# Three-block model, last block: gates and outputs with tokens on partitions, tanh gates in the recurrent layer, and down projections over both activation parts at once

## The chip, the cores and the metric

The kernel runs on one core of one Trainium2 chip. The metric is device microseconds of one execution, the median of several runs. TensorE (PE) multiplies, its weight loads (PEld) overlap it; VectorE (DVE), ScalarE (ACT), GpSimd (POOL) and SyncE (SP, which issues most of the loads) work beside it.

## What is computed

One sequence of 256 tokens (272 with 16 meta tokens in the first part) and 1024 channels, in float32, passes through three blocks. The first has an attention layer and a gated linear recurrent layer; the second has two hybrid layers (sparse attention, a long convolution, a short one, three gates, a feed-forward part with a convolution); the third has retention and block attention behind two sigmoid gates, and a feed-forward part of 2816 channels. What the change touches:

```python
# recurrent layer of block 1
r = jax.nn.sigmoid(jnp.einsum('btgi,gij->btgj', ub, w_rg).reshape(B, T, LRU_WIDTH) + b_rg)
i = jax.nn.sigmoid(jnp.einsum('btgi,gij->btgj', ub, w_ig).reshape(B, T, LRU_WIDTH) + b_ig)
log_a = -LRU_C * r.astype(jnp.float32) * jax.nn.softplus(-lam.astype(jnp.float32))
a = jnp.exp(log_a)
mult = jnp.sqrt(-jnp.expm1(2.0 * log_a))
...
b = mult * (i * uc).astype(jnp.float32)
...
# feed-forward part of block 2, both layers
return x + (jax.nn.silu(u_gate) * u_val) @ w_down
...
# block 3
ret = jax.nn.silu(rg) * retention(rq, rk, rv)
a = ret @ w_ret_out[l]
...
b = moba_attention(mq, mk, mv) @ w_moba_out[l]
mix = jax.nn.sigmoid(ga) * a + jax.nn.sigmoid(gb) * b
x = x + mix @ w_o[l]
h2 = rmsnorm_3(x, norm2_w[l])
f = (jax.nn.silu(h2 @ w_ffn_gate[l]) * (h2 @ w_ffn_up[l])) @ w_ffn_down[l]
x = x + f
```

## The kernel before

**Products in three parts.** Every large product is made of float32 numbers split in two: a high part in TensorE's fp32r format and the low rest. `mm3` adds up high weight x high activation, low x high and high x low, three matmuls for each 128 channels of the contraction (one step of k). Weights arrive in units of at most 1024 columns (`raw`, a load that SP issues); `emit_unit` makes the high part `whi` on ACT (L175) and the low part `wlo` on DVE (L181). Units are emitted three ahead of their use (`AHEAD = 3`, five buffers each). Activations are split in the same way by `split` (L157, L158) and `split_scaled` (L161, L162).

**Two forms of a product.** In the channel form (`tile_fm`, `part`) a 128 x 128 piece of the weight is loaded into TensorE and the activation streams through, with 256 columns (tokens; 272 in block 1); one output tile has 128 channels on partitions and takes one PSUM bank. In the token form (`tok_group`, `proj_tok`) 128 tokens of the activation are loaded and 512 columns of the weight stream; a group makes 512 channels for both halves of the tokens and takes two banks. Seven banks rotate. The hybrid layers' gates and outputs are in the token form; there `to_fm` turns a result back with TensorE transposes, four for a pair of channel tiles, and `mixture` does that while other matmuls run. In block 3 the projections `w_t3` are in the token form; the gates `w_g3`, the outputs `w_mo` and `w_ro`, and `w_o3` are in the channel form.

**What sets the order.** One stream of instructions is written out by hand; generators (norms, attention, the recurrence) are started with `spawn` and stepped by `tick`, once per eight steps of k times a rate; `drain` runs a generator to its end. The Tile scheduler then orders each engine's queue; `late` pins an instruction, and each engine runs its queue in order.

**Places that the change touches.** `lru()`: `block` (gate activations, L719), `gates` (exp, tanh and the input multiply, L709 to L712), the square root (L725), `conv4`, `chain` (L740 to L747: rr, the multiply on POOL L743, the scan), and `gated` (L766). Its products are `w_b_in` (16 tiles), `w_b_g` (4 units) and `w_b_out`; `yh`, `yl` are the parts of the activation of `w_b_out`. Tables of functions are loaded on ACT before a function of another table. `hybrid()` ends with `ffn` and a `residual` over `w_dn`, 8 tiles of 22 steps of k, whose activation parts are `fh` and `fl`. `third()`: `norm` makes the norm's scale per token (`rcol`) and, as a row over all partitions, `rb`; `retain` computes one head of the retention and turns it back (`rt`, L1466) into `rT`; the gate loop; `residual` over `w_o3`; `ffn`; and the last projection `w_d3`, with the addition (L1546) and the store of each tile.

The loop of the gates before:

```python
for m in range(8):
    o = self.tile_fm("w_g3", 16 - 8 * b + m, 8, xs, T)
    g = self.small("g3")[:, :T]
    dve.tensor_mul(g, o, rb)
    act.activation(g, g, AF.Sigmoid)
    ...
    o = self.tile_fm(wn, m, kt, ys, T)
```

Of the kernel before, what the change touches and what calls it, by code (L numbers as in the profile page):

```python
# [18 lines left out]
T = 256  # L19
# [36 lines left out]
class _Null:  # L56
# [14 lines left out]
    def __exit__(self, *a):  # L71
        return False


class Prog:
# [142 lines left out]
    def tile_fm(self, name, m, kt, xs, t):  # L218

        o = self.acc()[:, :t]  # L220
        for k0 in range(0, kt, 8):
            k1 = min(kt, k0 + 8)
            self.part(o, self.unit(name, m, k0 * 128, (k1 - k0) * 128), xs, k0, k1, kt, k0)
        return o

# [198 lines left out]
    def decay_rate(self):  # L424
# [19 lines left out]
        v.tensor_scalar_mul(self.spm8, al, -8.0)  # L444
        v.tensor_scalar_mul(self.sp4, al, 4.0)
# [228 lines left out]
    def residual(self, name, kt, xs, x, t, t0, gains, g2=None, lead=(2, 6), between=None):  # L674
# [8 lines left out]
        first = self.lead_fm(name, range(nl), xs, n, lead[1], between)  # L683
        for m in range(8):
            o = next(first) if m < nl else self.tile_fm(name, m, kt, xs, n)
            src = x[:, m, t0:]
            dve.tensor_add(src, o, src)
# [7 lines left out]
    def lru(self):  # L695
# [10 lines left out]
        def gates(g):  # L706

            for i in (2 * g, 2 * g + 1):
                self.late(act.activation(aa[:, i], rr[:, i], AF.Exp,  # L709
                                         scale=self.spm8[:, i:i + 1]))  # L710
                last[0] = act.activation(rr[:, i], rr[:, i], AF.Tanh, scale=self.sp4[:, i:i + 1])
                dve.tensor_mul(ii[:, i], ii[:, i], uc[:, i])  # L712

        def block(g):
            for c, o in self.tiles_of_unit("w_b_g", g, 4, 2,
                                           lambda k: (uh[:, 2 * g + k], ul[:, 2 * g + k]), T1):
                i = 2 * g + c % 2
                dst, b = (rr, "b_b_rg") if c < 2 else (ii, "b_b_ig")
                self.late(act.activation(dst[:, i], o, AF.Sigmoid, bias=self.v(b, i)))  # L719
            if g % 2:  # L720
# [4 lines left out]
                self.after(act.activation(rr[:, c], rr[:, c], AF.Sqrt), last[0])  # L725
# [196 lines left out]
    def hybrid(self, layer):  # L922
# [339 lines left out]
        fz = [(self.big("fh", 8, T, F32R), self.big("fl", 8, T, F32R)) for _ in range(3)]  # L1262
# [11 lines left out]
        def finish(og, ou, i):  # L1274
# [4 lines left out]
            self.split(fz[i // 8][0][:, i % 8], fz[i // 8][1][:, i % 8], u)  # L1279
# [3 lines left out]
        self.residual("w_dn_" + L, 22, lambda k: (fz[k // 8][0][:, k % 8], fz[k // 8][1][:, k % 8]),  # L1283
                      x, T, 0, nxt)
# [34 lines left out]
    def third(self):  # L1319
# [15 lines left out]
        def group(g):  # L1335
# [6 lines left out]
            self.proj_tok("w_t3", g, 512, dst)  # L1342
# [86 lines left out]
        rT = self.big("rT", 8, T)  # L1429

        def retain(hd):
# [32 lines left out]
            for i in range(2):  # L1464
                for j in range(2):
                    te.transpose(pt[:, i * 256 + j * 128:i * 256 + j * 128 + 128],  # L1466
                                 y[:, j * 256 + i * 128:j * 256 + i * 128 + 128], self.ident)
            act.activation(rT[:, 2 * hd:2 * hd + 2], pt.rearrange("p (a t) -> p a t", a=2),
                           AF.Copy)
# [10 lines left out]
        def norm():  # L1480
            yield
            self.norm_cols("n31")
            yield
            return (yield from self.rows(self.rcol, SEG2, "rb31"))

        job = self.spawn(norm(), 0.7)
        group(0)
        group(1)
        rb = self.drain(job)
# [9 lines left out]
        gr = self.big("gr", 8, T)  # L1499
        for m in range(8):  # L1500
            o = self.tile_fm("w_g3", m, 8, xs, T)
            dve.tensor_mul(gr[:, m], o, rb)
# [4 lines left out]
        def gated():  # L1507
            for m in range(8):
                dve.tensor_mul(rT[:, m], rT[:, m], gr[:, m])
                self.split(rT_h[:, m], rT_l[:, m], rT[:, m])  # L1510
                yield

        mg = self.big("mg3", 8, T)
# [196 lines left out]
```

## Time and profile before

| | |
|---|---|
| median of 3 runs | 1733.04 us (1731.53 to 1735.68) |
| profiled execution | 1733.38 us, of which the span is 1731.3 us |
| PE busy | 1709.9 us, 99%, 12215 matmuls |
| PEld busy | 1622.9 us, 94% |
| DVE busy | 1365.5 us, 79% |
| ACT busy | 1068.0 us, 62% |
| POOL busy | 61.7 us, 4% |
| HBM | 293.96 MB read, 170 GB/s over the span |

Busy time is the time in which at least one instruction of the engine ran. Matmuls are pipelined, so that one starts long before the last has ended; the pace of TensorE is the step from one start to the next. Instructions are named by line, engine, operation and out<-in in the program's names. The time in brackets behind an instruction is the idle time of its engine just before it, with what ended it. The granted clock is the share of 2.4 GHz that TensorE was given.

### The profile page before, as it was taken

What the parts mean: (1) busy time and instruction counts of PE and PEld (TensorE: products, weight loads), DVE (VectorE), ACT (ScalarE), POOL (GpSimd) and SP (SyncE); (2) the same over time, 40 slices, a digit from 0 to 9 for tenths busy, and PEclk for the clock granted to TensorE, in tenths of its full rate; (3) what the DMA queues carried; (4) which work ended last, traced back from release to release, by engine and by line L of the source; (5) the groups of instructions that cost most, each with busy time, mean ns of one, the idle gap of its engine ahead of it and who ended that gap; (6) DMA issues with size and microseconds to landing.
All of it is one profiled execution on the core that took longest, in us unless ns stands there. A gap on an engine that the chain in (4) does not pass through costs nothing.

```text
span 1731.3 us, 31869 instructions
## 1 busy us (share of the span) xinstructions
PE 1709.9 (99%) x12215; PEld 1622.9 (94%) x12215; DVE 1365.5 (79%) x2943; ACT 1068.0 (62%) x1808; POOL 61.7 (4%) x92
## 2 busy tenths in 40 slices
PE   9999899999999999999999999999999999999999
PEld 8999899998888999999999888999998789999999
DVE  7769998998997998667998898898757677786553
ACT  5667775677656776546578557576545756455442
POOL 1000100000000000000000000000000000000000
PEclk9999999999999999999999999999999999999999
DMA  7425465776775555667686775656665436656563
GB/s 271 135 71 170 133 204 177 218 221 195 230 227 176 191 180 181 184 175 210 190 228 196 214 222 189 202 171 197 186 191 187 146 96 187 189 163 196 184 184 97
DMA packets 91545, 318.64 MB, mean 184 GB/s; under 512 B 10448, under 2 KB 11616, under 8 KB 91392
## 3 DMA queue, kind: packets, MB, share of 16 engines
q1 hardware_dynamic: 84384, 292.51, 53.1%
q0 software_dynamic: 7008, 24.09, 7.0%
q8 instruction: 96, 1.57, 0.4%
q14 instruction: 57, 0.47, 0.1%
HBM read 293.96 MB, written 1.05 MB: 170 GB/s over the span
## 4 chain that ended last, share of the span: by engine, by line
PE 92%; ACT 3%; DVE 2%; issue 1%; DMA 1%; SPq 0%; DVEq 0%; POOLq 0%; ACTq 0%
PE acc L205 22%; PE acc L207 22%; PE acc L206 21%; PE tok L207 7%; PE tok L205 7%; PE tok L206 7%; DVE wlo L181 1%; ACT whi L175 1%; PE lg L1115 1%; PE ix L1070 1%; PE po L1108 1%; DMA wlo<-raw 1%; ACT ca L1234 0%; DMA raw<-w_a_in 0%; PE pt L913 0%
## 5 line engine op out<-in xcount | busy, mean ns | idle before, releaser
L175 ACT ACTIVATE whi<-raw 128x1024 fp32r<-128x1024 f32 (+3 forms) x573 | 586.4, 1027 | 417.1 <-PE acc L207 170.3
L181 DVE TENSOR_TENSOR wlo<-raw,whi 128x1024 fp32r<-128x1024 f32 (+3 forms) x531 | 628.3, 1186 | 203.6 <-ACT whi L175 199.3
L205 PE MATMUL acc<-bh,whi 128*128 128x256 f32 x1600 | 459.1, 288 | 0.0
L206 PE MATMUL acc<-bh,wlo 128*128 128x256 f32 x1600 | 451.7, 283 | 0.0
L207 PE MATMUL acc<-bl,whi 128*128 128x256 f32 x1600 | 451.2, 283 | 0.0
L205 PEld LDWEIGHTS acc<-bh,whi 128*128 128x128 f32 x1600 | 306.8, 192 | 2.7 <-issue 1.4
L206 PEld LDWEIGHTS acc<-bh,wlo 128*128 128x128 f32 x1600 | 306.6, 192 | 2.2 <-issue 0.7
L207 PEld LDWEIGHTS acc<-bl,whi 128*128 128x128 f32 x1600 | 306.1, 192 | 0.2 <-DVE bl L158 0.2
L979 DVE SCALAR_TENSOR_TENSOR ca<-apad,vec,ca 128x226 f32<-128x226 f32 (+14 forms) x480 | 195.9, 460 | 0.3
L206 PE MATMUL acc<-ah,wlo 128*128 128x256 f32 (+1 forms) x528 | 151.5, 287 | 6.1 <-DVE wlo L181 6.1
L205 PE MATMUL acc<-ah,whi 128*128 128x256 f32 (+1 forms) x528 | 153.3, 290 | 1.5 <-ACT ah L161 1.1
L207 PE MATMUL acc<-al,whi 128*128 128x256 f32 (+1 forms) x528 | 151.5, 287 | 0.0
L205 PE MATMUL acc<-fh,whi 128*128 128x256 f32 x528 | 149.4, 283 | 0.0
L206 PE MATMUL acc<-fh,wlo 128*128 128x256 f32 x528 | 149.4, 283 | 0.0
L207 PE MATMUL acc<-fl,whi 128*128 128x256 f32 x528 | 149.4, 283 | 0.0
L206 PEld LDWEIGHTS acc<-ah,wlo 128*128 128x128 f32 x528 | 101.2, 192 | 7.1 <-DVE wlo L181 7.0
L205 PEld LDWEIGHTS acc<-ah,whi 128*128 128x128 f32 x528 | 101.2, 192 | 2.3 <-ACT ah L161 1.3
L205 PE MATMUL tok<-whi,ah 128*128 128x424 f32 (+1 forms) x272 | 102.7, 377 | 0.0
L205 PEld LDWEIGHTS acc<-fh,whi 128*128 128x128 f32 x528 | 101.4, 192 | 0.0
L206 PEld LDWEIGHTS acc<-fh,wlo 128*128 128x128 f32 x528 | 101.4, 192 | 0.0
L207 PEld LDWEIGHTS acc<-fl,whi 128*128 128x128 f32 x528 | 101.4, 192 | 0.0
L207 PEld LDWEIGHTS acc<-al,whi 128*128 128x128 f32 x528 | 101.1, 192 | 0.2 <-DVE al L162 0.2
(559 smaller groups left out, 3332.8 us busy)
## 6 DMA issues: line engine op xcount, KB each, us to landing
raw<-w_up SPq DMA_DIRECT2D x88, 512.0 KB, 3.9
raw<-w_g SPq DMA_DIRECT2D x72, 512.0 KB, 4.4
raw<-w_c SPq DMA_DIRECT2D x48, 512.0 KB, 4.5
raw<-w_f SPq DMA_DIRECT2D x44, 512.0 KB, 3.6
wlo<-raw POOLq DMA_DIRECT2D x36, 512.0 KB, 6.6
raw<-w_t SPq DMA_DIRECT2D x40, 424.0 KB, 3.2
raw<-w_a SPq DMA_DIRECT2D x32, 512.0 KB, 4.4
raw<-w_dn SPq DMA_DIRECT2D x32, 512.0 KB, 3.6
```

Source lines behind the costliest of these rows:

```text
L175: nc.scalar.activation(hi[:, c], raw[:, c], AF.Copy)
L181: nc.vector.tensor_sub(lo[:, c], raw[:, c], hi[:, c].bitcast(F32))
L205: mm(out, wh, xh, start=start, stop=False)
L206: mm(out, wl, xh, start=False, stop=False)
L207: mm(out, wh, xl, start=False, stop=stop)
L979: tap = dve.scalar_tensor_tensor(ca[:, i, d:], ga[:, i, :T - d], w(i, j), ca[:, i, d:], op0=ALU.mult, op1=ALU.add)
L1070: te.matmul(ps[:, n * 2 * nk:(n + 1) * 2 * nk].rearrange("p (h k) -> p h k", h=2), kiT[:, 2 + i, q], kiT[:, 6:8, :nk], start=True, stop=True)
L1108: te.matmul(po, tok[k][:, 584 + g * 128:584 + (g + 1) * 128], ptb[:, k * n:(k + 1) * n], start=k == 0, stop=k == j)
L1115: te.matmul(ps[:, i * nk:(i + 1) * nk], qT[:, h, q], kiT[:, g, :nk], start=True, stop=True)
```

## The change

It has three parts.

In `lru()` the two sigmoids are written as tanh of half the argument. `spm8` and `sp4` are halved and serve as scale and bias, the square root takes a scale of 0.25, the first token's multiplier is 0.5, and the input multiply adds 1. The multiply by rr in `chain` moves from POOL to DVE.

For the three projections with 22 steps of k (`w_dn` in both hybrid layers, `w_d3`) the activation's high and low part lie beside each other (`Pairs`), so that the high weight takes both in one matmul of 512 columns; the low weight takes the high part with 256. The output has two halves in one bank, which are added to x one after the other.

In `third()` the gates `w_g3` and the outputs `w_mo` and `w_ro` get the token form (their weights are laid out anew on the host). The norm's scale is applied on ACT per token (`rcol`), so `rb` and its row matmuls go. `retain` writes the token-major `ry`, and `gated` multiplies and turns it back with `to_fm`; the mixture `mg` is turned back by `mixture`, during the last output groups and, for the last four channel tiles, between the two halves of the first four tiles of `w_o3` (`lead=(4, 4)`).

```diff
+class Pairs:
+    def __init__(self, prog, name, t):
+        self.a = [prog.big(name + "%d" % i, 8, t, F32R) for i in range(2)]
+    def __call__(self, k):
+        i = 2 * (k % 4)
+        return self.a[k // 4][:, i:i + 2]
...
+    def wide_part(self, o, unit, xs, k0, k1, kt, base=0):
+        wh, wl = unit
+        mm = self.nc.tensor.matmul
+        for k in range(k0, k1):
+            x = xs(k)
+            c = slice((k - base) * 128, (k - base + 1) * 128)
+            mm(o, wh[:, c], x, start=k == 0, stop=k == kt - 1, skip_group_check=True)
+            mm(o[:, 0], wl[:, c], x[:, 0], start=False, stop=k == kt - 1, skip_group_check=True)
+        self.tick((k1 - k0) / 8)
...
-        v.tensor_scalar_mul(self.spm8, al, -8.0)
-        v.tensor_scalar_mul(self.sp4, al, 4.0)
+        v.tensor_scalar_mul(self.spm8, al, -4.0)
+        v.tensor_scalar_mul(self.sp4, al, 2.0)
+        self.hb = cp.tile([128, 16], F32, name="hb")
+        v.tensor_scalar_mul(self.hb, self.v("b_b_rg", 0, 16), 0.5)
...
         for m in range(8):
-            o = next(first) if m < nl else self.tile_fm(name, m, kt, xs, n)
             src = x[:, m, t0:]
+            if wide:
+                o = next(first) if m < nl else self.wide_fm(name, m, kt, xw, n)
+                dve.tensor_add(src, o[:, 1], src)
+                o = o[:, 0]
+            else:
+                o = next(first) if m < nl else self.tile_fm(name, m, kt, xs, n)
             dve.tensor_add(src, o, src)
...
-                self.late(act.activation(aa[:, i], rr[:, i], AF.Exp,
-                                         scale=self.spm8[:, i:i + 1]))
-                last[0] = act.activation(rr[:, i], rr[:, i], AF.Tanh, scale=self.sp4[:, i:i + 1])
-                dve.tensor_mul(ii[:, i], ii[:, i], uc[:, i])
+                s8, s4 = self.spm8[:, i:i + 1], self.sp4[:, i:i + 1]
+                self.late(act.activation(aa[:, i], rr[:, i], AF.Exp, scale=s8, bias=s8))
+                last[0] = act.activation(rr[:, i], rr[:, i], AF.Tanh, scale=s4, bias=s4)
+                dve.scalar_tensor_tensor(ii[:, i], ii[:, i], 1.0, uc[:, i], op0=ALU.add,
+                                         op1=ALU.mult)
...
-                self.late(act.activation(dst[:, i], o, AF.Sigmoid, bias=self.v(b, i)))
+                self.late(act.activation(dst[:, i], o, AF.Tanh, scale=0.5,
+                                         bias=self.hb[:, b + i:b + i + 1]))
...
-                self.after(act.activation(rr[:, c], rr[:, c], AF.Sqrt), last[0])
+                self.after(act.activation(rr[:, c], rr[:, c], AF.Sqrt, scale=0.25), last[0])
...
-                dve.memset(rr[:, i, 0:1], 1.0)
-                pool.tensor_mul(ii[:, i], ii[:, i], rr[:, i])
+                dve.memset(rr[:, i, 0:1], 0.5)
+                dve.tensor_mul(ii[:, i], ii[:, i], rr[:, i])
...
-            y = self.half_k("gny")
             for j in range(2):
-                c = slice(j * 256, j * 256 + 256)
-                act.activation(y[:, c], po[:, c], AF.Identity, scale=r[:, j:j + 1],
-                               bias=nm[:, j:j + 1])
-            yield
-            pt = self.acc("rt")
...
+                act.activation(ry[:, j, e], po[:, j * 256:j * 256 + 256], AF.Identity,
+                               scale=r[:, j:j + 1], bias=nm[:, j:j + 1])
...
-            return (yield from self.rows(self.rcol, SEG2, "rb31"))
...
+                dve.tensor_mul(ry[:, :, c], ry[:, :, c], gr[:, :, c])
                 yield
+                self.to_fm(ry, m, rT_h, rT_l)
...
+            for g in range(2):
+                c = slice(g * 512, g * 512 + 512)
+                o = self.tok_group("w_g3", 4 - 2 * b + g, 8, xs)
+                sgs = [self.half_k("sgt") for _ in range(2)]
+                for j in range(2):
+                    act.activation(sgs[j], o[j], AF.Sigmoid, scale=self.rcol[:, j:j + 1])
...
+                if b == 1 and g == 0:
+                    self.drain(rjob)
+                    rjob = self.spawn(self.mixture(mg, mixed, mh, ml))
+                o = self.tok_group(wn, g, kt, ys)
...
+        self.residual("w_o3", 8, lambda k: (mh[:, k], ml[:, k]), x, T, 0, ["norm2_w_3"],
+                      lead=(4, 4), between=lambda: self.drain(rjob))
...
         for m in range(8):
-            o = self.tile_fm("w_d3", m, 22,
-                             lambda k: (fz[k // 8][0][:, k % 8], fz[k // 8][1][:, k % 8]), T)
-            dve.tensor_add(x[:, m], o, x[:, m])
+            o = self.wide_fm("w_d3", m, 22, lambda k: fz[k // 8](k % 8), T)
+            dve.tensor_add(x[:, m], o[:, 1], x[:, m])
+            dve.tensor_add(x[:, m], o[:, 0], x[:, m])
             nc.sync.dma_start(self.out[:, m], x[:, m])
```

PE's queue at the end of the last projection, the last two steps of k, before:

```order
L205 MATMUL acc<-fh,whi 128x256
L206 MATMUL acc<-fh,wlo 128x256
L207 MATMUL acc<-fl,whi 128x256
L205 MATMUL acc<-fh,whi 128x256
L206 MATMUL acc<-fh,wlo 128x256
L207 MATMUL acc<-fl,whi 128x256
L1703 UNCONDITIONAL_BRANCH
```

The same place after the change:

```order
L250 MATMUL acc<-f_17488,whi 128x512
L251 MATMUL acc<-f_17488,wlo 128x256
L250 MATMUL acc<-f_17488,whi 128x512
L251 MATMUL acc<-f_17488,wlo 128x256
L1771 UNCONDITIONAL_BRANCH
```

Two matmuls stand for three, the first of twice the width.

DVE's queue in the recurrent layer, between the low weight parts of two tiles of `w_b_in`, before (uc<-aa,ii is the scan, gy<-acc the eviction of a gate tile):

```order
L181 TENSOR_TENSOR wlo<-raw,whi 128x1024
L740 SCALAR_TENSOR_TENSOR rr<-aa,rr 128x272
L771 TENSOR_TENSOR gy<-acc,nb_1932 128x256
L742 MEMSET rr 128x1
L740 SCALAR_TENSOR_TENSOR rr<-aa,rr 128x272 x2
L742 MEMSET rr 128x1
L747 SCALAR_TENSOR_TENSOR uc<-aa,ii 128x272
L774 SCALAR_TENSOR_TENSOR gy<-th,gy 128x256
L747 SCALAR_TENSOR_TENSOR uc<-aa,ii 128x272
L742 MEMSET rr 128x1
L740 SCALAR_TENSOR_TENSOR rr<-aa,rr 128x272
L181 TENSOR_TENSOR wlo<-raw,whi 128x1024
```

The same stretch after the change:

```order
L197 TENSOR_TENSOR wlo<-raw,whi 128x1024
L832 TENSOR_TENSOR gy<-acc,nb_1934 128x256
L801 SCALAR_TENSOR_TENSOR rr<-aa,rr 128x272 x2
L803 MEMSET rr 128x1
L801 SCALAR_TENSOR_TENSOR rr<-aa,rr 128x272
L804 TENSOR_TENSOR ii<-ii,rr 128x272
L803 MEMSET rr 128x1 x2
L808 SCALAR_TENSOR_TENSOR uc<-aa,ii 128x272
L835 SCALAR_TENSOR_TENSOR gy<-th,gy 128x256
L832 TENSOR_TENSOR gy<-acc,nb_1934 128x256
L804 TENSOR_TENSOR ii<-ii,rr 128x272
L197 TENSOR_TENSOR wlo<-raw,whi 128x1024
```

Two multiplies (ii<-ii,rr) and a second eviction stand in it now; one scan and one rr have moved behind the second wlo, ahead of the first `yl`.

PE's queue in the first half of `w_o3` after the change, where the last eight transposes of `mg` stand between the fourth and the fifth step of k of the leading tiles:

```order
L221 MATMUL acc<-mh,whi 128x256
L222 MATMUL acc<-mh,wlo 128x256
L223 MATMUL acc<-ml,whi 128x256
L919 MATMUL tr<-ident,mg_16575 128x128 x8
L221 MATMUL acc<-mh,whi 128x256
L222 MATMUL acc<-mh,wlo 128x256
```

Before, the outputs `rT` were followed by the matmuls of `w_o3` alone.

## Rows read from the trace of the kernel before

**Rows 1.** The page: busy us (share) and instructions; chain that ended last.

```profile
PE 1709.9 (99%) x12215; PEld 1622.9 (94%) x12215; DVE 1365.5 (79%) x2943; ACT 1068.0 (62%) x1808; POOL 61.7 (4%) x92
PE 92%; ACT 3%; DVE 2%; issue 1%; DMA 1%; SPq 0%; DVEq 0%; POOLq 0%; ACTq 0%
```

**Rows 2.** Groups (xcount, busy us, mean ns) and timeline (start us, us), last projection.

```profile
L205 PE MATMUL acc<-fh,whi 128*128 128x256 f32 x528 | 149.4, 283 | 0.0
...
1664.11 0.28 PE L205 MATMUL acc<-fh,whi 128*128 128x256 f32 x1
...
1727.35 0.28 PE L207 MATMUL acc<-fl,whi 128*128 128x256 f32 x1
```

**Rows 3.** Timeline, PE, two token groups of a hybrid layer, 48 matmuls, ends.

```profile
478.75 0.39 PE L206 MATMUL tok<-whi,ol 128*128 128x512 f32 x1
...
489.40 0.39 PE L205 MATMUL tok<-whi,bh 128*128 128x512 f32 x1
```

**Rows 4.** Windows: stretch, us, busy of PE, PEld, DVE, ACT, POOL; PEclk; DMA.

```profile
140.00:216.00 76.00, 68.96 (x538) 67.47 (x537) 68.97 (x151) 57.46 (x95) 7.84 (x8) 0.98 0.46 145
```

**Rows 5.** Timeline, PE waits in the recurrent layer; then a window there.

```profile
185.18 0.38 PE L206 MATMUL acc<-ah,wlo 128*128 128x256 f32 x1 [1.88 <-DVE wlo L181]
...
204.17 0.39 PE L206 MATMUL acc<-ah,wlo 128*128 128x256 f32 x1 [3.05 <-DVE wlo L181]
...
210.73 0.39 PE L207 MATMUL acc<-yl,whi 128*128 128x256 f32 x1 [1.26 <-DVE yl L162]
...
186.00:200.00 14.00, 14.00 (x108) 14.00 (x108) 11.02 (x23) 13.77 (x22) 0.83 (x1) 0.89 0.60 186
```

**Rows 6.** Timeline, DVE: two operations in a row; the last addition.

```profile
155.78 0.78 DVE L158 TENSOR_TENSOR ul<-uc,uh 128x272 fp32r<-128x272 f32 x2
...
1727.66 0.42 DVE L1546 TENSOR_TENSOR x<-acc,x 128x256 f32<-128x256 f32 x1 [7.49 <-PE acc L207]
```

**Rows 7.** Groups of PE from 1398.46 to 1512.85 us, gates and outputs.

```profile
L205 PE MATMUL acc<-ah,whi 128*128 128x256 f32 x192 | 55.3, 288 | 0.0
...
L205 PE MATMUL acc<-rTh,whi 128*128 128x256 f32 x64 | 18.1, 283 | 0.0
...
L205 PE MATMUL acc<-bT,whi 128*128 128x256 f32 x32 | 9.1, 285 | 0.0
```

**Rows 8.** Timeline, PE, four transposes of the retention among matmuls.

```profile
1428.40 0.28 PE L207 MATMUL acc<-al,whi 128*128 128x256 f32 x1
1428.52 0.60 PE L1466 MATMUL rt<-ident,gny 128*128 128x128 f32 x4
1428.88 0.36 PE L205 MATMUL acc<-ah,whi 128*128 128x256 f32 x1
1429.08 0.28 PE L206 MATMUL acc<-ah,wlo 128*128 128x256 f32 x1
```

**Rows 9.** Timeline, PE, the row broadcast of block 3's first norm.

```profile
1318.04 0.61 PE L312 MATMUL rb31rp<-rb31dg,ones 128*128 128x128 f32 x4
```

**Rows 10.** Groups from 176 to 212 us; then timeline of POOL and DVE.

```profile
L181 DVE TENSOR_TENSOR wlo<-raw,whi 128x1024 fp32r<-128x1024 f32 x9 | 12.0, 1332 | 0.0
...
L740 DVE SCALAR_TENSOR_TENSOR rr<-aa,rr 128x272 f32<-128x272 f32 x8 | 5.0, 647 | 0.8 <-ACT rr L725 0.8
...
L771 DVE TENSOR_TENSOR gy<-acc,nb 128x256 f32<-128x256 f32 x8 | 3.3, 418 | 2.9 <-PE acc L207 2.9
...
202.16 0.88 POOL L743 TENSOR_TENSOR ii<-ii,rr 128x272 f32<-128x272 f32 x1 [1.02 <-DVE rr L742]
...
202.34 1.77 DVE L181 TENSOR_TENSOR wlo<-raw,whi 128x1024 fp32r<-128x1024 f32 x1
...
204.38 1.21 DVE L181 TENSOR_TENSOR wlo<-raw,whi 128x1024 fp32r<-128x1024 f32 x1
```

**Rows 11.** Timeline, ACT, recurrent layer: exp, tanh and a table load.

```profile
167.52 0.53 ACT L709 ACTIVATE aa<-rr,spm 128x272 f32<-128x272 f32 x1
...
168.27 0.51 ACT L711 ACTIVATE rr<-rr,sp 128x272 f32<-128x272 f32 x1
...
183.90 1.28 ACT L709 ACT_TABLE_LOAD   x1
```

More of the change, by code (lines that the diff above doesn't have):

```diff
@@ L224, in tile_fm, with wide_fm, wide_lead @@
         return o
+    def wide_part(self, o, unit, xs, k0, k1, kt, base=0):
[7 more added lines that the diff above has]
+        self.tick((k1 - k0) / 8)
+    def wide_fm(self, name, m, kt, xs, t):
+        o = self.acc()[:, :2 * t].rearrange("p (a t) -> p a t", a=2)
+        for k0 in range(0, kt, 8):
+            k1 = min(kt, k0 + 8)
+            self.wide_part(o, self.unit(name, m, k0 * 128, (k1 - k0) * 128), xs, k0, k1, kt, k0)
+        return o
+    def wide_lead(self, name, ms, xs, t, ks, between=None):
+        os = [(self.acc()[:, :2 * t].rearrange("p (a t) -> p a t", a=2),
+               self.unit(name, m, 0, 1024)) for m in ms]
+        for o, u in os:
+            self.wide_part(o, u, xs, 0, ks, 8)
+        if between:
+            between()
+        for o, u in os:
+            self.wide_part(o, u, xs, ks, 8, 8)
+            yield o
     def lead_fm(self, name, ms, xs, t, ks, between=None):
@@ L1259, in hybrid @@
                       [("norm2_g_2", layer)], lead=(4, 4), between=lambda: self.drain(job))
-        fz = [(self.big("fh", 8, T, F32R), self.big("fl", 8, T, F32R)) for _ in range(3)]
+        fz = [Pairs(self, "f", T) for _ in range(3)]
         def conv3(o, c):
@@ L1333, in third, with group @@
         t1 = [self.big("t1_%d" % j, 1, 2048)[:, 0] for j in range(2)]
-        def group(g):
+        os = []
+        def group(g, wait=True):
             if g < 4:
@@ L1341, in group, with evict @@
                 dst = lambda j: rv[:, j, (g - 5) * 512:(g - 4) * 512]
-            self.proj_tok("w_t3", g, 512, dst)
+            os.append((self.tok_group("w_t3", g, 8, xs), dst))
+            if wait:
+                evict(g)
+        def evict(g):
+            o, dst = os[g]
+            for j in range(2):
+                act.activation(dst(j), o[j], AF.Copy, scale=self.rcol[:, j:j + 1])
             done[0] = g + 1
@@ L1482, in norm @@
             self.norm_cols("n31")
[L1483 to L1484 removed]
         job = self.spawn(norm(), 0.7)
[L1487 removed]
+        group(0, wait=False)
+        self.drain(job)
+        evict(0)
         group(1)
[L1489 removed]
         ajob = self.spawn(attention(), 1.2)
@@ L1497, in third @@
         rjob = self.spawn(self.stagger([retain(i) for i in range(4)], 3), 1.0)
[L1499 to L1502, printed above, removed]
+        gr = self.big("gr", 2, 1024)
+        for g in range(2):
+            o = self.tok_group("w_g3", g, 8, xs)
+            for j in range(2):
+                act.activation(gr[:, j, g * 512:g * 512 + 512], o[j], AF.Copy,
+                               scale=self.rcol[:, j:j + 1])
         self.drain(ajob)
@@ L1536, in finish @@
+                mixed[0] = b * (g + 1)
+        self.residual("w_o3", 8, lambda k: (mh[:, k], ml[:, k]), x, T, 0, ["norm2_w_3"],
+                      lead=(4, 4), between=lambda: self.drain(rjob))
+        fz = [Pairs(self, "f", T) for _ in range(3)]
         def finish(og, ou, i):
```

67 lines of the change are left out of this document (31 added, 36 removed).

## Prediction

> **What bounds the kernel now.** The page's busy list comes first [rows 1]: TensorE is busy for 1709.9 of the 1731.3 us and DVE for 1365.5. The second line there, the chain of work that ended last, puts 92% of the span on PE. So the time is, nearly everywhere, the number of matmuls times the step from one start to the next, and other engines matter only where PE stands still for them. The busy share itself is no measure of speed, since the matmuls overlap (283 ns each by the page [rows 2], yet one starts every 120 ns); the steps are read from starts in the timeline.
>
> The step comes next. In the last down projection the 528 matmuls of 256 columns start between 1664.11 and 1727.35 us without a gap [rows 2]: 63.24 / 527 = 0.1200 us a step. With 512 columns, in the token-on-partition groups of the hybrid layers, 47 steps take 489.40 - 478.75 us [rows 3]: 0.2266 us, 0.2267 below. Twice the columns thus cost 0.1067 us more, and 0.0133 us of every step is there whatever the width. A pair of 256-column matmuls (0.2400) that becomes one of 512 gives back 0.0133 us.
>
> Last, the places where PE stands still and which the change touches. In the stretch from 140 to 216 us, which holds the recurrent layer, PE is busy for 68.96 of 76 us and DVE for 68.97 [rows 4]. PE's rows there [rows 5] wait 1.88 and 3.05 us for `wlo`, the low part of a weight that DVE makes, and 1.26 us for `yl`. In 186 to 200 us the granted clock is 0.89 (a part of that at the lower level, 1.2 of 2.4 GHz), right after the 1.88 us wait; 0.11 x 14 us = 1.5 us more. After the 3.05 us wait it did not fall.
>
> **The change part by part.** *Down projections.* Per step of k there are now three matmuls of 256 columns, 0.3600 us. Afterwards one of 512 (the high weight on both activation parts) and one of 256 (the low weight), 0.2267 + 0.1200 = 0.3467. There are 3 projections x 8 tiles x 22 steps = 528 steps (the page's x528 of [rows 2]); all lie on the path. 528 x 0.0133 = **-7.0 us**. The evictions double (two additions instead of one, both on DVE), 24 additions at about 0.36 us, hidden by the 7.6 us of the next tile. Only the very last one is not: x of the last tile is ready one addition later, **+0.35** (one such addition takes 0.42 alone, two operations of that kind in a row 0.78 [rows 6], so 0.36 for one more).
>
> *Last block, gates and outputs.* Before, 192 + 64 + 32 matmuls of 256 columns for each of the three products [rows 7], 864 in all. Afterwards the activations are the loaded side and the weights stream at 512 columns: 432 matmuls. 432 x 0.0133 = **-5.8 us**. Weights, bytes and splits are the same in amount.
>
> *Transposes.* Token-major results have to be turned back. 16 transposes of the retention's output go, 16 of `ry` and 16 of `mg` come: 16 more. Four of them between two matmuls of 256 columns shift the start of the second matmul behind from 0.24 to 1429.08 - 1428.40 = 0.68 us [rows 8]: 0.44 us for four, 0.11 each. 16 x 0.11 = **+1.8 us**. The row broadcast of the first norm (`rb31`, four short matmul records [rows 9]) goes; by the price of four transposes **-0.4**.
>
> *Cover of the new transposes.* The last eight of `mg` stand, after the change, behind 48 matmuls of w_o3 (48 x 0.12 = 5.8 us). That hides four DVE operations of 512 columns on the last outputs, under 0.7 us each by the 1.21 us of 1024 columns [rows 10]: 2.8 us at most, ahead of the first of the eight transposes. Without that cover they would cost 2.8 us. I take nothing, with +3 as the bad end. The gates' evictions move to ACT with a scale per token and get fewer (16 small DVE multiplies and 16 sigmoids become 8 sigmoids of twice the width), so no engine has more to do there.
>
> *Recurrent layer.* The sigmoids become tanh, which lies in one table with exp: aa (exp) at 167.52 and rr (tanh) at 168.27 follow with no load between [rows 11]. Three loads like the one at 183.90 go, 3 x 1.28 = 3.8 us of ACT. That is not on PE's path by itself; it lets the square root, and with it DVE's chain of rr, ii and uc, begin earlier. DVE decides here. It gains eight multiplies that GpSimd did: 8 x 0.36 = +2.9 us. It loses what GpSimd did to it: while GpSimd multiplies (202.16), the wlo at 202.34 takes 1.77 us against 1.21 for the one at 204.38. The group rows show the same: rr L740 has a mean of 647 ns and wlo 1332 [rows 10]. That is 0.5 us for each of the eight, -4.0 to -4.5. Of its waits in that stretch, 2.9 us for PE and 0.8 for ACT [rows 10], I let half go, since DVE is behind PE more often afterwards: -1.8. DVE reaches the first `yl` some 3 us sooner. But DVE is still the later one: in the new order a multiply and one more eviction stand ahead of the second late wlo, and a multiply, a scan and an rr ahead of the first `yl`. PE gets to its last wait earlier and stands longer there, and a fall of the clock as above would take 1.5 us back. Bounds: -5 (all waits and the fall gone) and +1 (the eight multiplies come on top, no wait goes, a second fall). I take **-2.5**, nearer to DVE's 3 us than to the middle.
>
> Sum: -7.0 + 0.35 - 5.8 + 1.8 - 0.4 - 2.5 = -13.5 us. The profiled execution took 1733.38 us, 2.1 more than its span; the median of the runs is 1733.04, 0.3 lower. 1733.04 - 13.5 = **1719.5 us**.
>
> **The rivals.** *The recurrent layer gives nothing or loses.* For it: DVE is as busy as PE there and gets more instructions; against it: the stretched rows. Then -11 to -10, 1722 to 1723.
>
> *The fixed part does not halve.* A 512-column matmul is followed in the down projections by a short one with other weights, a mix that no row shows; if the short one had to wait for its weights, or if the 13 ns belonged to something other than the matmul, the 12.8 us would shrink. By [rows 2, 3] it is part of every step, and the groups of [rows 3] load weights for each matmul too. The Trainium skill (TensorE: Matmul & The Clock Gate, section Back-to-back issue gap) gives columns / 2.4 GHz + 2.5 ns for matmuls back to back, so only 2.5 ns would be saved on each of the 960: 2.4 us. This trace does not agree (13.3 ns beyond columns / 2.4 GHz at both widths). If only a fifth of the gain came, the sum would be -13.5 + 10.4, 1729.9.
>
> *Slower: the two-bank groups make PE wait.* A token group holds two accumulators until ACT or DVE, busy with weight splits, have emptied them, and seven are in rotation with the transposes. It costs one wait per group, 10 groups from the first gate to the last output; from 13.5 / 10 = 1.35 us per group on it decides, and at 1.7 us a group the time is 1733.04 - 13.5 + 17 = 1736.5. Against it: the same form runs in the hybrid layers with no gap over the 47 steps of [rows 3], across the border between two groups.
>
> *It does not do what it says*: the tanh form might keep its loads; the built order has four loads in that stretch instead of seven, so no.
>
> **How the numbers follow.** Forecast (-16 to -12) 0.64; recurrent layer without gain 0.22; a few us of new waits in the last block (1725 to 1729) 0.06; fixed part stays 0.05; slower 0.03. What a measurement of this kernel can tell from no change is about 0.2%, 3.5 us. Faster 0.93 (the forecast, the recurrent layer without gain, the new waits, and a hundredth of the fixed-part case), same 0.04 (the rest of that case), slower 0.03. The range takes the recurrent layer from -5 to +1, the cover's +3 and the spread of the runs: 1714.5 to 1726.
>
> **What would show it.** In the profile after: the f matmuls of 512 and 256 columns with a step of 0.347 us for two, 61.0 us instead of 63.4 for the last projection; the stretch from the first gate to w_o3 some 3.5 us shorter, with no wait over 0.5 us ahead of the `mg` transposes; wlo in the recurrent stretch at 1.2 us throughout, rr near 0.43, and less time between the first late wlo and `yl`. Wrong if the two-matmul step is over 0.355 us, if `tok` matmuls of the last block wait for ACT or DVE, or if PE waits over 8 us in the recurrent layer.

## The result and the profile after

The changed kernel takes 1722.88 us (median of 4 runs, 1721.77 to 1723.06); the kernel before took 1733.52 us beside it (4 runs, 1731.53 to 1735.68). The ratio is 0.9939, with a 95% interval of 0.9928 to 0.9951: faster by 10.6 us. The forecast was 1719.5 us, 13.5 less than before. Direction and range held; the gain is some 3 us smaller than forecast.

The profiled execution after took 1721.77 us with a span of 1720.0, 11.3 less than the span before; it lies 1.1 us under the median of the runs. From its page come the busy engines and the chain of work that ended last, as in [rows 1], and the two groups that take the place of the groups of [rows 2]:

```profile
PE 1702.6 (99%) x11267; PEld 1573.6 (91%) x11267; DVE 1360.3 (79%) x2922; ACT 1064.5 (62%) x1784; POOL 53.8 (3%) x84
...
PE 91%; ACT 4%; DVE 2%; DMA 1%; issue 1%; SPq 0%; POOLq 0%; ACTq 0%; DVEq 0%
...
L250 PE MATMUL acc<-f,whi 128*128 128x512 f32 x528 | 186.7, 399 | 0.0
L251 PE MATMUL acc<-f,wlo 128*128 128x256 f32 x528 | 148.3, 281 | 0.0
```

PE is still busy 99% of the span and the chain still runs on it. Of the 11.3 us, 7.3 are busy time of PE and 4.0 idle time; PE's waits in the recurrent layer (7.0 us before and 2.9 after, from 176 to 212 us) make up nearly all of the idle part. Where the 11.3 us come from is split with seven starts. Timeline of PE, kernel before: first matmul of the recurrent layer's gates, of its output projection, of the first hybrid layer, of the last block, of the retention, of w_o3 and of the last feed-forward part.

```profile
155.75 0.29 PE L205 MATMUL acc<-uh,whi 128*128 128x272 f32 x1
206.97 0.28 PE L205 MATMUL acc<-yh,whi 128*128 128x256 f32 x1
233.14 0.36 PE L205 MATMUL tok<-whi,ah 128*128 128x424 f32 x1
1301.23 0.40 PE L205 MATMUL tok<-whi,ah 128*128 128x512 f32 x1
1402.61 0.38 PE L1433 MATMUL rs<-qkT 128*128 128x256 f32 x1
1512.90 0.28 PE L205 MATMUL acc<-mh,whi 128*128 128x256 f32 x1
1535.94 0.28 PE L205 MATMUL acc<-ah,whi 128*128 128x256 f32 x1
```

The same places in the timeline of the changed kernel:

```profile
155.54 0.29 PE L221 MATMUL acc<-uh,whi 128*128 128x272 f32 x1
199.76 0.28 PE L221 MATMUL acc<-yh,whi 128*128 128x256 f32 x1
228.33 0.36 PE L221 MATMUL tok<-whi,ah 128*128 128x424 f32 x1
1294.31 0.40 PE L221 MATMUL tok<-whi,ah 128*128 128x512 f32 x1
1395.17 0.38 PE L1502 MATMUL rs<-qkT 128*128 128x256 f32 x1
1501.24 0.28 PE L221 MATMUL acc<-mh,whi 128*128 128x256 f32 x1
1525.41 0.28 PE L221 MATMUL acc<-ah,whi 128*128 128x256 f32 x1
```

The differences of neighbouring starts, after less before:

| stretch | before, us | after, us | difference |
|---|---|---|---|
| up to the gates | 155.75 | 155.54 | -0.2 |
| recurrent layer up to its output projection | 51.22 | 44.22 | -7.0 |
| that projection | 26.17 | 28.57 | +2.4 |
| two hybrid layers (with two of the down projections) | 1068.09 | 1065.98 | -2.1 |
| last block up to the retention | 101.38 | 100.86 | -0.5 |
| retention, gates, outputs | 110.29 | 106.07 | -4.2 |
| w_o3 | 23.04 | 24.17 | +1.1 |
| from there to the end of the span | 195.4 | 194.6 | -0.8 |

The last row holds the third down projection (-1.2) and the added addition behind the last matmul (+0.4). The last projection itself, timeline of PE in the changed kernel:

```profile
1653.57 0.40 PE L250 MATMUL acc<-f,whi 128*128 128x512 f32 x1
1653.80 0.28 PE L251 MATMUL acc<-f,wlo 128*128 128x256 f32 x1
1653.92 0.40 PE L250 MATMUL acc<-f,whi 128*128 128x512 f32 x1
1654.16 0.28 PE L251 MATMUL acc<-f,wlo 128*128 128x256 f32 x1
1654.28 0.40 PE L250 MATMUL acc<-f,whi 128*128 128x512 f32 x1
1654.52 0.28 PE L251 MATMUL acc<-f,wlo 128*128 128x256 f32 x1
1654.63 0.40 PE L250 MATMUL acc<-f,whi 128*128 128x512 f32 x1
...
1715.64 0.28 PE L251 MATMUL acc<-f,wlo 128*128 128x256 f32 x1
```

Three steps of k (a 512-column and a 256-column matmul each) take 1654.63 - 1653.57 = 1.06 us, 0.3533 a step. The forecast was 0.3467 and the step before was 0.3600, so half of the gain came. The starts in the trace repeat every third step: 241 and 120 ns, 236 and 113, 232 and 118. From first to last start it is 62.07 us where [rows 2] have 63.24.

The recurrent layer, windows of the changed kernel (columns as in [rows 4]), then PE's two waits behind 200 us in its timeline:

```profile
140.00:216.00 76.00, 72.96 (x577) 71.88 (x576) 69.22 (x164) 56.14 (x96) 0.00 (x0) 0.98 0.49 157
...
200.00:212.00 12.00, 9.01 (x56) 8.21 (x55) 11.85 (x28) 3.99 (x9) 0.00 (x0) 0.86 0.47 163
...
201.37 0.38 PE L222 MATMUL acc<-yh,wlo 128*128 128x256 f32 x1 [0.45 <-DVE wlo L197]
...
204.67 0.39 PE L223 MATMUL acc<-yl,whi 128*128 128x256 f32 x1 [2.49 <-DVE yl L178]
```

The waits of 1.88 and 3.05 us for `wlo` in [rows 5] are gone. The wait for `yl` grew from 1.26 to 2.49 us, and the lower level of the clock (1.2 GHz) stands behind it now (0.86 over the 12 us: 1.7 us lost) instead of in 186 to 200 us. GpSimd does nothing in the stretch any more. DVE's groups from 176 to 212 us (count, busy us, mean ns), which answer to [rows 10]:

```profile
L197 DVE TENSOR_TENSOR wlo<-raw,whi 128x1024 fp32r<-128x1024 f32 x11 | 13.3, 1215 | 0.0
...
L801 DVE SCALAR_TENSOR_TENSOR rr<-aa,rr 128x272 f32<-128x272 f32 x8 | 3.3, 436 | 0.6 <-ACT rr L786 0.6
```

`wlo` fell from 1332 to 1215 ns and `rr` from 647 to 436.

In the last block, the last eight transposes of `mg`, PE's timeline:

```profile
1506.87 0.28 PE L223 MATMUL acc<-ml,whi 128*128 128x256 f32 x1
1506.99 1.03 PE L919 MATMUL tr<-ident,mg 128*128 128x128 f32 x8
1507.79 0.36 PE L221 MATMUL acc<-mh,whi 128*128 128x256 f32 x1
1507.99 0.28 PE L222 MATMUL acc<-mh,wlo 128*128 128x256 f32 x1
1508.28 0.38 PE L221 MATMUL acc<-mh,whi 128*128 128x256 f32 x1
```

They start 0.12 us after the matmul ahead of them, so the 48 matmuls of w_o3 do cover the outputs' last DVE work. They move the next matmul by 0.80 us, and one more hole of 0.17 follows (1508.28 - 1507.99 = 0.29 where 0.12 is the rule).

### The profile page after: what moved, and what is told of

It is laid out like the page before. It is cut to its first block, busy times and chain, and to the rows that moved or that the text cites. A ratio compares the mean times of both kernels' runs of the same rounds, so it can differ in the third digit from the quotient of the medians.

```text
span 1720.0 us, 29882 instructions
## 1 busy us (share of the span) xinstructions
PE 1702.6 (99%) x11267; PEld 1573.6 (91%) x11267; DVE 1360.3 (79%) x2922; ACT 1064.5 (62%) x1784; POOL 53.8 (3%) x84
## 4 chain that ended last, share of the span: by engine, by line
PE 91%; ACT 4%; DVE 2%; DMA 1%; issue 1%; SPq 0%; POOLq 0%; ACTq 0%; DVEq 0%
PE acc L221 16%; PE acc L223 16%; PE acc L222 16%; PE tok L223 9%; PE tok L221 9%; PE tok L222 9%; PE acc L250 7%; PE acc L251 4%; DVE wlo L197 1%; ACT whi L191 1%; PE lg L1176 1%; PE ix L1131 1%; PE po L1169 1%; DMA wlo<-raw 1%; ACT ca L1295 0%
## 5 line engine op out<-in xcount | busy, mean ns | idle before, releaser
L250 PE MATMUL acc<-f,whi 128*128 128x512 f32 x528 | 186.7, 399 | 0.0
L251 PE MATMUL acc<-f,wlo 128*128 128x256 f32 x528 | 148.3, 281 | 0.0
L221 PE MATMUL tok<-whi,ah 128*128 128x512 f32 (+1 forms) x368 | 141.2, 384 | 0.0
L223 PE MATMUL tok<-wlo,ah 128*128 128x512 f32 (+1 forms) x368 | 138.4, 376 | 0.0
L222 PE MATMUL tok<-whi,al 128*128 128x512 f32 (+1 forms) x368 | 137.9, 375 | 0.0
L250 PEld LDWEIGHTS acc<-f,whi 128*128 128x128 f32 x528 | 99.2, 188 | 24.6
L251 PEld LDWEIGHTS acc<-f,wlo 128*128 128x128 f32 x528 | 99.7, 189 | 0.0
L221 PE MATMUL acc<-ah,whi 128*128 128x272 f32 (+1 forms) x336 | 97.9, 291 | 1.3 <-ACT whi L191 1.3
L222 PE MATMUL acc<-ah,wlo 128*128 128x272 f32 (+1 forms) x336 | 97.1, 289 | 1.0 <-DVE wlo L197 1.0
L223 PE MATMUL acc<-al,whi 128*128 128x272 f32 (+1 forms) x336 | 96.8, 288 | 0.0
```

Source lines behind the costliest of these rows:

```text
L221: mm(out, wh, xh, start=start, stop=False)
L222: mm(out, wl, xh, start=False, stop=False)
L223: mm(out, wh, xl, start=False, stop=stop)
L250: mm(o, wh[:, c], x, start=k == 0, stop=k == kt - 1, skip_group_check=True)
L251: mm(o[:, 0], wl[:, c], x[:, 0], start=False, stop=k == kt - 1, skip_group_check=True)
```

## The experiments

**One part at a time.** Three kernels each hold the kernel before and one part of the change, to see whether the parts add. The first has the joined down projections alone: the pair class for the activations, the two matmuls a step and the two additions.

> The kernel before with the joined down projections alone (528 steps of a 512-column and a 256-column matmul). Additive theory with the step as the profile after shows it (353 ns a step instead of 360): 528 x -0.0067 + 0.35 = -3.2 us, time about 1730. If the lost half belongs to something else in the changed kernel (its other two parts) and the pair takes 347 ns here: -6.7 us, about 1726.5. If the pair saves nothing by itself: within 0.5 us of the kernel before.

The second has the recurrent layer's part alone:

```
-  self.late(act.activation(dst[:, i], o, AF.Sigmoid, bias=self.v(b, i)))
+  self.late(act.activation(dst[:, i], o, AF.Tanh, scale=0.5, bias=self.hb[:, b + i:b + i + 1]))
...
-  pool.tensor_mul(ii[:, i], ii[:, i], rr[:, i])
+  dve.tensor_mul(ii[:, i], ii[:, i], rr[:, i])
```

> The kernel before with the recurrent layer's change alone (gates by tanh, the multiply of ii and rr on DVE instead of GpSimd). If its landmarks in the profile after are its own: -4.6 us (uh to yh -7, yh to the next stage +2.4), about 1728.5. If part of that gain is chance in the start-up of the program: -2.5 or less, 1730.5 or more.

The third has the last block's gates, outputs and transposes alone:

```
-  o = self.tile_fm("w_g3", 16 - 8 * b + m, 8, xs, T)
+  o = self.tok_group("w_g3", 4 - 2 * b + g, 8, xs)
```

> The kernel before with the last block's gates and outputs with tokens on partitions, nothing else. By the landmarks of the profile after: first product of the block to the first retention score -0.5, from there to w_o3 -4.2, w_o3 itself +1.1, sum -3.6 us, about 1729.5. By the prediction's terms (432 x -0.0133 + 1.8 - 0.4): -4.4, about 1728.7, with w_o3 unchanged in length. If the evictions of two-bank groups held PE: 0 or more.

All three ran beside the same kernel before (1732.8 us):

| part alone | time, us | ratio, 95% interval | difference |
|---|---|---|---|
| down projections | 1729.68 | 0.9985, 0.9976 to 0.9994 | -3.1 |
| recurrent layer | 1728.94 | 0.9979, 0.9970 to 0.9988 | -3.9 |
| last block | 1728.28 | 0.9977, 0.9967 to 0.9986 | -4.5 |

The sum is -11.5 us, and together the parts gave -10.6: within the noise they add. The first case of each expectation is the nearer one for the down projections and the recurrent layer. Each down projection alone is again 1.17 us shorter, so the half that is missing is missing in the part itself. For the last block the medians don't decide (-4.5, with an interval from -5.7 to -2.4 that holds both cases); the starts do: -0.6 up to the retention, -4.2 to w_o3 and +1.1 in it, as in the changed kernel, the first case.

**Where the down projections' half went.** Same products and counts; only the order within a weight unit differs, all 512-column matmuls first, then all of 256 columns:

```
-  for k in range(k0, k1):
-      mm(o, wh[:, c], x, ...)
-      mm(o[:, 0], wl[:, c], x[:, 0], ...)
+  for k, c in cs:
+      mm(o, wh[:, c], xs(k), ...)
+  for k, c in cs:
+      mm(o[:, 0], wl[:, c], xs(k)[:, 0], ...)
```

> The changed kernel with the matmuls of each weight unit in another order: first all 512-column ones (high weight), then all 256-column ones (low weight); same products, same count. If the lost 6.7 ns a step come from the change of width at every matmul: two changes a unit instead of sixteen, step about 347 to 348 ns (61.1 us from first to last f matmul of the last projection), 1722.9 - 3.1 = 1719.8. If they belong to the 512-column matmul itself in this form (weights of 128 columns against a strided or longer stream): 353 ns and 1722.9, and all 512-column steps show 233 to 241 ns in a row. If they belong to the 256-column one: its steps in a row stay at 120 and the 512-column ones at 226.7, which is the first case again, so only the two sizes read apart decide between the first two.

1720.08 us, 0.9932 (0.9919 to 0.9944), against the 1719.8 of the first case. Timeline of PE in the last projection of this kernel, where a row stands for several matmuls of one form (start of the first, and their number):

```profile
1657.26 1.12 PE L251 MATMUL acc<-f,wlo 128*128 128x256 f32 x8
1658.21 1.55 PE L249 MATMUL acc<-f,whi 128*128 128x512 f32 x6
1659.60 0.64 PE L251 MATMUL acc<-f,wlo 128*128 128x256 f32 x4
```

Eight 256-column matmuls take 1658.21 - 1657.26 = 0.95 us (8 x 0.12 = 0.96). Six of 512 columns right behind them take 1659.60 - 1658.21 = 1.39, where 6 x 0.2267 is 1.36. So a way from one width to the other and back costs about 20 ns, and a unit of eight steps has one such way now instead of eight. Each projection is 1.87 us shorter than before (1.17 in the changed kernel). The step comes to 0.349, a little over the 347 to 348 expected, since I had priced every change of width at half of the 6.7 ns that a pair cost when it alternated; with several of a kind in a row a way there and back costs more than one alternating pair. By this run it is the change of width. The next run takes the change away altogether: the low weight, too, is multiplied by both activation parts. That is a fourth product, which the reference doesn't need, and makes all matmuls 512 wide.

```
-  mm(o[:, 0], wl[:, c], x[:, 0], start=False, ...)
+  mm(o, wl[:, c], x, start=False, ...)
```

> The changed kernel with the low weight, too, multiplied by both activation parts (a fourth product that the reference's arithmetic does not need): down projections of 512-column matmuls only, weights changed at each. If the change of width costs the 6.7 ns a step: no change of width, 2 x 226.7 = 453.3 ns a step, last projection 176 x 0.4533 = 79.8 us from first to last. If the 512-column matmul in this form costs 6.7 ns more by itself: 466.7 ns a step, 82.1 us. Whole time about 1722.9 + 528 x 0.100 = 1775.9 in the first case, 1783 in the second.

Timeline of PE, last projection, first and last matmul:

```profile
1688.22 0.40 PE L250 MATMUL acc<-f,whi 128*128 128x512 f32 x1
...
1767.80 0.39 PE L251 MATMUL acc<-f,wlo 128*128 128x512 f32 x1
```

79.58 us over 351 steps is 0.2267 us, the step of [rows 3]. The 512-column matmul of a pair of activation parts with 128-column weights costs nothing extra; the mix does. The kernel ran once and took 1774.06 us, near the first case (1775.9); the reading rests on the starts.

**What in the recurrent layer gave the gain.** The layer's part has two edits. In this kernel, otherwise the changed one, the multiply of `ii` and `rr` is back on GpSimd:

```
-  dve.tensor_mul(ii[:, i], ii[:, i], rr[:, i])
+  pool.tensor_mul(ii[:, i], ii[:, i], rr[:, i])
```

> The changed kernel with the multiply of ii and rr in the recurrent layer back on GpSimd; gates by tanh stay. If GpSimd slowing DVE down is the larger half of the layer's gain (the prediction: 0.5 us for each of eight, less 0.36 us that the multiply costs DVE): +1.5 to +3 us against the changed kernel, 1724.5 to 1726, with wlo and rr rows in 185 to 205 us stretched to 1.7 and over 0.6 us again. If the saved table loads carry the gain: within 0.7 us of 1722.9, since DVE is then relieved of eight multiplies for the stretching.

1723.89 us, 0.9950 (0.9936 to 0.9963). Between the first gate matmul and the first hybrid layer it takes 73.57 us, 0.8 more than the changed kernel (72.79); the time is 1.0 us longer, between the two cases. Its timeline shows PE's first wait, then both engines' price, first GpSimd and then DVE beside it, then PE's second wait:

```profile
183.08 0.39 PE L222 MATMUL acc<-ah,wlo 128*128 128x256 f32 x1 [0.24 <-DVE wlo L197]
...
194.78 1.76 POOL L804 TENSOR_TENSOR ii<-ii,rr 128x272 f32<-128x272 f32 x2 [8.04 <-DVE rr L803]
...
194.90 1.00 DVE L801 SCALAR_TENSOR_TENSOR rr<-aa,rr 128x272 f32<-128x272 f32 x1
...
195.83 1.30 DVE L808 TENSOR_TENSOR_SCAN uc<-aa,ii 128x272 f32<-128x272 f32 x1
...
199.58 0.38 PE L222 MATMUL acc<-ah,wlo 128*128 128x256 f32 x1 [2.05 <-DVE wlo L197]
```

An `rr` beside the two multiplies takes 1.00 us instead of 0.44 and a scan 1.30 instead of 0.71, and PE stands 2.05 us for a `wlo` again. The Trainium skill (SBUF — State Buffer, section SBUF: two separate sides) says that GpSimd and a DVE operation with two operands in SBUF share one pair of ports, of which one holds the whole and the other waits; these rows agree (1.00 against 0.44 us, 1.30 against 0.71). The opposite edit, in the kernel before: the multiply alone goes to DVE, the sigmoids stay.

> The kernel before with one line changed: the multiply of ii and rr on DVE instead of GpSimd; gates by sigmoid stay, with their table loads. If GpSimd slowing DVE down is the larger half of the gain of the layer: -2 to -3 us, 1730 to 1731. If the saved table loads carry it: 0 to +1.5 us (eight more DVE instructions, the square root as late as before), 1733 to 1734.5. With the run before this one the two should add to about -3.9 us; if both alone give nearly the whole, they remove the same wait.

1730.26 us, 0.9987 (0.9978 to 0.9996), -2.2 us, as the first case says; by the starts the stretch is 74.35 us, 3.0 less than the 77.39 before. The waits of PE from 176 to 212 us by what they were for, in this kernel (us in all, times, longest):

```profile
PE acc L207 <- DVE yl L162: 2.2, 2, 1.8
PE acc L206 <- DVE wlo L181: 1.6, 2, 1.3
```

By the starts tanh alone shortens the stretch by 3.8 us, the multiply alone by 3.0, both by 4.6. In each of these four profiles one lower stretch of the clock of the same length falls into the layer. But in two more profiles of the layer with both edits (the part alone, and the changed kernel once more, below) the lower stretch is twice as long and the layer takes 73.46 and 73.82 us, so that such a stretch is good to 1 us only. The times don't decide whether the edits add: the run with tanh alone gains 8.5 us over the kernel before that ran beside it, the changed kernel 10.6, with intervals that overlap; by that the multiply would be worth 2.1 us beside tanh and 2.2 alone. What repeats is when DVE starts its first `yl`. These rows are of the kernel before, tanh alone, the multiply alone and the changed kernel:

```profile
209.76 0.91 DVE L162 SCALAR_TENSOR_TENSOR yl<-gy,yh 128x256 fp32r<-128x256 f32 x1
204.54 0.42 DVE L178 SCALAR_TENSOR_TENSOR yl<-gy,yh 128x256 fp32r<-128x256 f32 x1
205.94 0.43 DVE L162 SCALAR_TENSOR_TENSOR yl<-gy,yh 128x256 fp32r<-128x256 f32 x1
204.19 0.42 DVE L178 SCALAR_TENSOR_TENSOR yl<-gy,yh 128x256 fp32r<-128x256 f32 x1
```

Less PE's first gate matmul in the same profile (155.75, 155.65, 156.18 and 155.54 us) that is 54.0, 48.9, 49.8 and 48.65 us. The last figure comes again to 0.01 us in the other five profiles whose layer has the same two edits and no other that touches DVE; the layer of before gives 54.05 and 53.3 in two more. So tanh alone brings `yl` forward by 5.1 us, the multiply alone by 4.3, both by 5.4. They aren't two gains that add: both work on the same waits. The first wait for `wlo` (1.88 us in [rows 5]) is 0.24 us with tanh alone and gone with the multiply alone; the second (3.05) is 2.05 and 1.26 us; and the 2.9 us that DVE stood for PE [rows 10] are gone in both. With tanh alone the two square roots start only 0.7 and 0.9 us sooner behind the first gate matmul. But ahead of the first late `wlo` just one DVE operation is stretched beside GpSimd (1.28 us), where before three are (1.03, 0.94 and 1.30 us).

**The wait that is left.** Two tries to take it away, both in the reordered kernel. In the first, the low parts of every second weight of the output projection are made by ACT and an accumulating DMA:

```
+  self.dma_share, self.share = 0.5, 0.5
   self.residual("w_b_out", 8, ...)
+  self.dma_share, self.share = 0.0, 0.0
```

> The reordered kernel (all 512-column matmuls of a unit, then all 256-column ones) and, in the recurrent layer's output projection, every second low weight part made by ACT and an accumulating DMA instead of DVE. Theory: the last wait of that layer (2.5 us for yl) and the half clock behind it (3.4 us at 1.2 GHz, 1.7 us lost) are there because DVE is late with yl by its queue, with two wlo of 1.22 us ahead of it that go: yl comes 2.4 us sooner, the wait falls under 0.6 us, the clock stays, -2 to -4 us against 1720.1, so 1716 to 1718. Rival: the accumulating DMAs or ACT (two more copies of 1.04 us, and GpSimd's queue) land late or slow DVE down, and PE waits for wlo instead: 1719.5 or more.

1720.98 us, 0.9932 (0.9920 to 0.9945): no gain over 1720.08, as the rival says. PE's timeline:

```profile
202.23 0.39 PE L221 MATMUL acc<-yh,whi 128*128 128x256 f32 x1 [1.96 <-ACT yh L177]
203.81 0.58 PE L222 MATMUL acc<-yh,wlo 128*128 128x256 f32 x1 [1.20 <-DMA wlo<-raw]
```

`yl` is no longer waited for, but ACT, with two more copies of 1.04 us ahead of `yh` in its queue, is late with `yh` by 1.96 us, and a DMA with a `wlo` by 1.20.

The second leaves the wait and takes away what follows it. Ten matmuls of the constant (20 records in the profile) fill it, and in the down projections every second unit takes its 256-column matmuls first, so that the widths change four times a tile and not six:

```
+  for low in ((1, 0) if k0 // 8 % 2 else (0, 1)):
...
   mm(o, wh[:, c], xh, start=True, stop=False)
+  self.fill(10, None)
   mm(o, wl[:, c], xh, start=False, stop=False)
```

> The reordered kernel, with two more edits: every second weight unit of a down projection runs its 256-column matmuls first (four changes of width a tile of x instead of six, so two pairs of matmuls fewer to pay for a change), and ten matmuls of a constant, whose result nothing reads, stand behind the first yh matmul of the recurrent layer's output projection, where PE would wait for yl. First edit: about 20 ns for each way there and back between the widths, 24 tiles x 20 ns = 0.5 us, a projection 61.2 us instead of 61.4. Second edit, theory: the half clock behind the wait (3.4 us in the reordered kernel's profile, 6.8 us in the run with the recurrent layer alone) falls away with the idle time, 1.7 us or more, and the stretch from the first yh matmul to the next stage is 26.9 us or less instead of 28.6; in all 1717.9. Rival: the fall doesn't come from that idle time, or the extra matmuls push the yh products back behind yl: the stretch stays 28.6 or grows by up to 2 us, 1719.6 to 1721.6.

1717.42 us (1717.21 to 1717.52), 0.9903 (0.9889 to 0.9916): faster than the kernel before and the changed one, and the fastest of this study. A window and PE's timeline:

```profile
200.00:212.00 12.00, 10.42 (x86) 10.06 (x85) 11.85 (x28) 4.04 (x9) 0.00 (x0) 1.00 0.49 163
...
199.91 2.39 PE L228 MATMUL fillps<-ones 128*128 128x128 f32 x20
...
204.72 0.39 PE L243 MATMUL acc<-yl,whi 128*128 128x256 f32 x1 [1.58 <-DVE yl L178]
```

The granted clock stays 1.00 (2.4 GHz) although PE still stands 1.58 us; `yl` is used 4.92 us after the first `yh` matmul, in the reordered kernel as here (204.61 - 199.69), so the fillers delay nothing. The projection's stretch is 27.36 us against 28.59 there, -1.2, less than the 1.7 expected: with PE at 2.4 GHz the trace shows four holes of 0.07 to 0.11 us behind 204.7, where the lower clock had covered DVE's pace. The down projections are 2.03 us shorter than before, each. By the spans the kernel gains 2.6 us on the reordered one: 1.2 and 0.5 by these two edits, and 1.0 in the hybrid layers beside the projections, which no edit touches and which take from 941.2 to 942.6 us in the twelve profiles. That the time came so near to the expected 1717.9 is in part luck. The clock is from one profile; that the four runs lie within 0.3 us, and the five of the reordered kernel within 1.9, fits it.

The changed kernel once more, on the same chip beside it:

> The changed kernel once more, beside the run above on the same chip. 1722.9 us as before, 5 us above the filled and reordered kernel by the theory, 3.3 us above it or less by its rival. Its down projections take 62.1 to 62.2 us again with the same three-step pattern of 241, 236 and 232 to 233 ns, since that pattern belongs to the order of the matmuls and not to chance; the place and the length of the half-clock stretch behind the wait for yl may differ from the first profile.

1723.43 us, 0.9940 (0.9926 to 0.9954), 6.0 us over the filled and reordered kernel. By the starts 2.6 of it are the down projections, 2.3 the recurrent layer's output projection, and 1.3 again the hybrid layers beside the projections. The down projections are again 1.17 us shorter than before, each. What differs from the first profile of the changed kernel is the clock; windows from 200 to 212 us in this run and, second, in the run of the last block's part, whose recurrent layer is that of the kernel before:

```profile
200.00:212.00 12.00, 9.01 (x48) 8.21 (x47) 11.85 (x28) 3.86 (x9) 0.00 (x0) 0.72 0.49 164
```

```profile
200.00:212.00 12.00, 9.18 (x48) 8.65 (x49) 11.37 (x22) 4.65 (x10) 1.99 (x2) 0.72 0.52 175
```

The lower stretch is twice as long as in the first profile of the changed kernel (0.72 against 0.86), and this projection takes 29.62 us instead of 28.57. And the recurrent layer of before has its lower stretch behind the first wait in one profile [rows 5], at the second in the other.

## Why the prediction was right, and where its sum was off

*The down projections* are the term that was mis-sized: -7.0 forecast, -3.5 by the starts (3 x 1.17), -3.1 as a part alone. The step that failed is the 0.2267 + 0.1200 for a pair: I read each duration from a row of equal neighbours and added them. The pair takes 0.3533. The prediction had named the doubt (a mix that no row shows) and put it under a rival in which the whole fixed part stays, at a price for all 960 matmuls; it was half of it, and for the 528 mixed pairs alone. The 0.3533 is only just under the 0.355 that the prediction named as a sign of being wrong. The all-512 run and the order of the units show that it is the mixing. The Trainium skill (TensorE: Matmul & The Clock Gate, section Back-to-back issue gap) gives columns / 2.4 + 2.5 ns as the gap of an isolated matmul, and about 131 ns for 512 columns in a sustained stream with weight loads; the rows here, 226.7 ns for 512 columns, 13.3 ns beyond columns / 2.4 at both widths and 6.7 ns more for a mixed pair, agree with neither.

*The last addition*: +0.35 forecast, +0.38 measured.

*The last block*: -5.8 + 1.8 - 0.4 = -4.4 forecast, -3.6 by the starts (-0.5, -4.2, +1.1). The mechanism held: no token group waits for an eviction, and four `ry` transposes cost 0.45 us, as those of [rows 8] did. The row broadcast gave its 0.4: the first gate matmul comes 97.23 us behind the start of the block before (1398.46 - 1301.23) and 96.81 after (1391.12 - 1294.31). Of the 0.8 us that are missing, 0.2 is the hole behind the last `mg` transposes. Some 0.3 is the mix of widths again: matmuls of the heads and transposes, with other widths, stand between the 512-column matmuls of the gates and outputs, and at the 12 places behind them the second to eighth 512-column steps together are on the mean 27 ns longer than seven of 0.2267 us. That is the size of the first steps in the reordered kernel; no run took these places away. The other 0.3 isn't tied to single rows.

*The cover of the last transposes*, taken at nothing, held.

*The recurrent layer*: -2.5 forecast, -4.6 by the starts (-7.0 + 2.4) of this profile, good to 1 us, and -3.9 as a part alone, nearer to the good bound. The picture was right in its order: the waits for `wlo` go, PE reaches its last wait earlier and stands longer there (2.49 against 1.26 us), and a fall of the clock costs 1.7 us at the new place. The size was off where I let half of DVE's own waits go (-1.8): of the 3.7 us of [rows 10] only 0.6 is left (the `rr` row after), and DVE starts its first `yl` 5.4 us sooner, not some 3. In both single runs DVE's 2.9 us for PE went together with PE's first wait, which suggests that DVE stood for PE because PE had stood for DVE. A sum of single durations on DVE doesn't show that.

*The rest*: -0.2 up to the recurrent layer and +0.2 in the hybrid layers beside the projections. With +0.38, -3.5, -3.6 and -4.6 that makes -11.3, the difference of the spans.

*The rivals.* Slower through two-bank groups didn't come, nor did a recurrent layer without gain. The forecast's errors, +3.5 and +0.8 on one side and -2.1 on the other, went against each other; that the time fell so well into the range is in part luck.

## What to carry to other kernels

A step read from a row of equal matmuls holds for equal neighbours: when an edit mixes widths, keep those of one width together, over a whole weight unit at least, or measure the mix first. Where two edits relieve the same engine ahead of the same wait, cost them together by that wait, not each by its own instructions. Where PE must stand at a late operand, matmuls without use that end before the operand is there can save the lower clock behind the wait (1.2 us here, at one place in one kernel).

## What was unexpected of the hardware

A 512-column matmul behind a 256-column one with other weights: 353.3 ns a pair in a pattern of three steps (241 and 120, 236 and 113, 232 and 118 ns), where each alone runs at 226.7 and 120.0. In the reordered kernel the first five 512-column starts behind a change are 233, 236, 228, 233 and 231 ns apart, then 226 to 227, and the first 256-column one behind them takes 113: the cost of a change is spread over the next matmuls and a part comes back. Why, no run here shows.

With the same code, and waits of 1.9 to 3.1 us, the granted clock fell at one wait in one execution and at another, or for twice as long, in the next. A profile of one execution prices such a stretch to 1 us only.
